# First MLP products as seven products of blocks, with three of four weight sums made by adding transfers

## The chip, the cores and the metric

The kernel runs on one core of a Trainium2 chip. The core has a matrix engine (TensorE, PE in the profile; its weight loads are listed as PEld), three engines for elementwise work (VectorE = DVE, ScalarE = ACT, GpSimd = POOL), and SyncE (SP), which here only issues transfers. Each engine works through its own instructions in the order of the program, and semaphores make one engine wait for another. Transfers issued by SP's queue are plain copies; POOL's queue can also issue adding transfers, which add what they fetch to what stands in SBUF. The metric is device time of one execution in microseconds.

## The reference

A two-layer encoder on x of 512 positions and 1024 features, in float32: layer 0 has stick-breaking attention, layer 1 an RG-LRU block, and each is followed by the same kind of MLP. Cut to the part that the change touches:

```python
def squared_relu_mlp(h, w1, w2):
    u = jax.nn.relu(h @ w1)          # 512x1024 @ 1024x4096
    return (u * u) @ w2              # 512x4096 @ 4096x1024
...
    h = rms_norm(x, norm_mlp[layer])
    x = x + squared_relu_mlp(h, mlp_w1[layer], mlp_w2[layer])
return rms_norm(x, norm_final)
```

## The kernel before

**Precision.** TensorE multiplies in a format shorter than float32 (float32r). So every operand is kept as a high part and a low part, `a = ah + al`: ScalarE copies it to the high part, which rounds it (the CAST of lines 197, 823 and 843), and VectorE subtracts that from the original for the low part (lines 204, 824, 844). One product is then three matmuls, high x high, high x low and low x high. In this text "cut" is that pair of operations on a block of weights, giving `wh` and `wl`, and "split" the same on u.

**The MLP.** Class `Mlp` handles one layer. The 4096 hidden features are done in four quarters of 1024 (`q4`, 0 to 3). Each quarter has a first product (x with w1, relu, square: u) and a second product (u with w2, added up in the four output tiles c0 to c3). x lies feature by position: `xgh` and `xgl` are the halves of x times the norm's factors. The norm's other factor, one number per position, is put in when results are collected (`rr`, line 888), so relu and square can run before it is known.

- First product, before: `squared(q4, c)` makes 128 features of u at a time: it fetches a slab of 512 KB of weights, cuts it, and does 8 x 3 matmuls of 512 columns (lines 209 to 211), 8 such per quarter.
- Second product: `down()` uses Strassen's scheme in Winograd's form: of 2 x 2 blocks it makes seven products P1 to P7 instead of eight, with sums of blocks as operands. A quarter has two pairs (units of 512 features, index g or p), so 14 products of 12 matmuls of 512 columns each (line 877). The sums of u are made by `sums()` (line 807) and split by `split()`; the sums of weights are made in place: P5 is b11+b12, P6 adds b22 to that, P7 is b12+b22, P4 adds b21 to P6's sum. VectorE adds them (line 865), except where a product stands in `far`: there POOL issues an adding transfer (line 858). Before, `far` has P7 and P4 in the last quarter of layer 0, P4 in the last of layer 1, and is empty elsewhere.
- `block()` forms the sum and `operand()` cuts it into `wh` and `wl`, which come from a pool of four buffers: an operand can be cut once the product four before it is done. `load()` fetches b11, b12 and b22 (two buffers each, one for each pair) on SP's queue; b21 is fetched where it is needed, into one of three raw buffers.
- u of two chunks stands in one tile (line 787) of which there is one buffer, so the next two chunks can write theirs only after the split; the splits go to `bh`/`bl` for the first pair and to `sh`/`sl` for the second.
- `quarters()` runs it all: the eight chunks of a quarter, then `down()`; the first two chunks of the next quarter are put ahead of `down()`.

**Order.** TensorE's order is that of the program text. The order on the other engines is chosen by a scheduler, when the program is built; once built, it is fixed. x of each layer stays in SBUF (`HOMES`) until the second product's output is added to it: in layer 0 by `feature()`, in layer 1 by transposes in `between()` in the last quarter (lines 1189 to 1195).

Of the kernel before, what the change touches and what calls it, by code (L numbers as in the profile page):

```python
# [14 lines left out]
ALU = mybir.AluOpType  # L15
# [33 lines left out]
def hybrid_encoder(  # L49
# [10 lines left out]
    w_m1: bass.AP,  # L60
    w_dn: bass.AP,
# [666 lines left out]
    class Mlp:  # L728
# [10 lines left out]

        PRODUCTS = {  # L740
            "P1": (0, "b11", None, "X", 0, False),
            "P5": (4, "b11", "b12", "V", 3, False),
            "P6": (5, "b11", "b22", "X", 1, True),
            "P3": (6, "b22", None, "V", 1, False),
            "P7": (1, "b12", "b22", "X", 3, True),
            "P2": (2, "b21", None, "W", 0, False),
            "P4": (3, "b11", "b21", "X", 2, False),
# [5 lines left out]
        def __init__(self, ctx, layer):  # L753
# [9 lines left out]
            self.u, self.raws = {}, {}  # L763
# [9 lines left out]
        def squared(self, q4, c, ready=None):  # L773

            if self.first is None:
                self.first = [self.bank() for _ in range(2)]
                ws = [slab(w_m1[self.layer, i]) for i in range(2)]
                beside(ws, xgh, xgl, self.first, {})
            if self.first:
                ps = self.first.pop(0)  # L780
            else:
                ps = dense(
                    w_m1[self.layer, q4 * C + c], xgh, xgl, halves=ready, ps=self.bank()
                )
            j, a = divmod(c, 2)
            if a == 0:
                self.u[j] = self.mp.tile([P, BLOCKS, HS], F32, tag="u", name="u", bufs=1)
            t = self.u[j][:, 2 * a : 2 * a + 2, :].rearrange("p i n -> p (i n)")
            A.activation(t, ps, AF.Relu)
            A.activation(t, t, AF.Square)  # L790
            if q4 == 0:

                if c in range(2, C - 2):
                    for i in range(2):
                        self.sq.chunk(2 * (c - 2) + i, x[2 * (c - 2) + i])
                if c == C - 1:
                    self.rr = self.sq.inv_squares(self.bank())
            return t

        def sums(self, j):  # L800

            u = self.u[j]
            for out, x, y, op in (
                (4, 1, 3, ALU.subtract), (5, 4, 0, ALU.subtract), (6, 5, 2, ALU.add),
                (1, 0, 1, ALU.subtract),
            ):
                V.tensor_tensor(u[:, out, :], u[:, x, :], u[:, y, :], op)  # L807

        def split(self, j):
            if j < 2:  # L810
                n = BLOCKS * HS
                h, l = (
                    t.rearrange("p c s -> p (c s)")[:, j * n : (j + 1) * n].rearrange(
                        "p (i n) -> p i n", n=HS
                    )
                    for t in (bh, bl)
                )
            else:
                h, l = (
                    self.bp.tile([P, BLOCKS, HS], F32R, tag=t, name=t) for t in ("sh", "sl")  # L820
                )
            u = self.u[j]
            A.copy(h, u)  # L823
            self.ready = V.tensor_tensor(l, u, f(h), ALU.subtract)  # L824
            self.a[j] = h, l

        def weights(self, q4, g, tag):
            return w_dn[self.layer, q4, g, *self.SOURCES[tag]]

        def load(self, q4):  # L830

            for g in range(2):
                for tag in ("b11", "b12", "b22"):
                    t = self.bp.tile([P, 2, S], F32, tag=tag, name=tag)
                    nc.sync.dma_start(out=t, in_=self.weights(q4, g, tag))
                    self.raws[tag, g] = t
# [10 lines left out]
        def block(self, q4, name, g, far):  # L847

            _, b, to, *_ = self.PRODUCTS[name]
            if b == "b21":  # L850
                t = wpool.tile([P, C, P], F32, tag="raw", name="raw", bufs=3)
                t = t.rearrange("p (j k) f -> p j (k f)", j=2)
                nc.sync.dma_start(out=t, in_=self.weights(q4, g, b))
                self.raws[b, g] = t
            raw = self.raws[b, g]
            if name in far:

                G.dma_start(out=raw, in_=self.weights(q4, g, to), accum_op=ALU.add)  # L858
            elif to:

                ahead = None
                if far and (name, g) != ("P5", 0):
                    ahead = self.ready if name == "P5" else self.before
                with tc.issue_after(ahead.ins) if ahead else nullcontext():
                    self.sum = V.tensor_tensor(raw, raw, self.raws[to, g], ALU.add)  # L865
            return self.operand(raw)

        def times(self, name, g, i, w, ps, new, cols=slice(0, S)):
# [4 lines left out]
            for jj in range(2):  # L873
                h, l = self.a[2 * g + jj]
                first, last = new and g == jj == 0, g == jj == 1
                for n, (x, y) in enumerate(((h, wh), (h, wl), (l, wh))):
                    PE.matmul(  # L877
                        ps, x[:, block, ts], y[:, jj, cols], start=first and n == 0,
# [14 lines left out]
        def down(self, q4, far=(), end=None):  # L893
            sums, last_cut = {}, {}

            def product(name, g, w=None):
                w = w or self.block(q4, name, g, far)
# [13 lines left out]
            if end is None:  # L911
                for name in ("P1", "P5", "P6", "P3", "P7", "P2", "P4"):
                    for g in range(2):
                        product(name, g)
# [414 lines left out]
```

## Time and profile before

| what | value |
| --- | --- |
| time, median of 3 runs | 1076.51 us (1075.07 to 1077.06) |
| the profiled execution: time / span | 1076.9 us / 1075.1 us |
| TensorE's granted clock, mean over the span | 0.997 |
| transfers, mean over the span | 117 GB/s |
| adding transfers in the MLPs / in layer 1's RG-LRU stage | 6 / 10 |
| MLP of layer 0 / layer 1, from the first quarter's second product to the end of the last | 304.4 to 576.4 us / 788.6 to 1075.1 us |

How to read it: busy time of an engine is the sum of its instructions; TensorE's matmuls are pipelined, so one lasts longer than the distance to the next, and a pace is read from the distance of starts. A row of the windows gives the stretch, then for each engine its busy time and count of instructions, the granted clock, the mean busy share of the 16 transfer engines and the GB/s moved. A row of a group gives line, engine, operation, `output<-inputs`, shapes, count, busy time, mean ns of one, then the idle time of the engine ahead of them and what ended it. A row of the timeline gives start, duration, engine, line and operation.

### The profile page before, as it was taken

To read this page: it belongs to the slowest core of one execution; us is meant where nothing else is said; L and a number is where in the kernel's file an instruction comes from. 1 tells how busy PE (TensorE), PEld (TensorE's weight loads), DVE (VectorE), ACT (ScalarE), POOL (GpSimd) and SP (SyncE) were. 2 spreads that over 40 slices of the span, in tenths; PEclk is the share of its full clock that TensorE was granted. 3 is DMA by queue.
4 is the path that set the end of the run, shared out by engine and by line. 5 is a ranking of instruction groups with operands and counts; after the bars stand their busy time and mean duration, and the time that the engine had idled before them with its cause. 6 is when DMAs were issued, how large, how long until landed. Compare 5 with 4: busy or idle time off the path is not lost.

```text
span 1075.1 us, 13570 instructions
## 1 busy us (share of the span) xinstructions
PE 1059.4 (99%) x5004; PEld 879.4 (82%) x5004; DVE 782.4 (73%) x1020; ACT 599.6 (56%) x888; POOL 166.8 (16%) x192
## 2 busy tenths in 40 slices
PE   9999999999999999999999999999999999999997
PEld 7888888888888888888878777888888888888875
DVE  7788787838686596597578878974676597497667
ACT  6777676826554543544546477944554544544346
POOL 2344443510000000000001655000000000000005
PEclk9999999999999999999999999999999999999999
DMA  7745454517215206206341785252215206305104
GB/s 236 198 117 148 122 147 108 170 52 249 85 49 187 79 31 187 96 20 191 84 98 60 180 211 129 87 191 82 79 43 190 82 22 189 103 20 176 59 6 112
DMA packets 44033, 125.70 MB, mean 117 GB/s; under 512 B 7744, under 2 KB 8512, under 8 KB 43968
## 3 DMA queue, kind: packets, MB, share of 16 engines
q1 hardware_dynamic: 41088, 115.94, 34.8%
q0 software_dynamic: 2304, 8.39, 4.5%
q8 instruction: 39, 0.64, 0.2%
q10 hardware_dynamic: 576, 0.52, 0.1%
q14 instruction: 26, 0.21, 0.1%
HBM read 104.91 MB, written 2.10 MB: 100 GB/s over the span
## 4 chain that ended last, share of the span: by engine, by line
PE 86%; DVE 5%; ACT 3%; issue 2%; POOL 2%; DMA 1%; SPq 0%; ACTq 0%; DVEq 0%; POOLq 0%
PE ps_t L877 8%; PE ps_acc L877 7%; PE ps_o L877 6%; PE ps_acc L211 6%; PE ps_acc L209 6%; PE ps_acc L210 6%; PE ps_z L877 5%; PE ps_t L209 4%; PE ps_t L210 4%; PE ps_t L211 4%; PE ps_o L209 4%; PE ps_o L211 4%; PE ps_o L210 4%; PE ps_z L210 3%; PE ps_z L211 3%; PE ps_z L209 3%
## 5 line engine op out<-in xcount | busy, mean ns | idle before, releaser
L204 DVE TENSOR_TENSOR wl<-raw,wh 128x1024 fp32r<-128x1024 f32 (+2 forms) x126 | 130.5, 1052 | 89.7 <-ACT wh L197 89.5
L843 ACT CAST wh<-b 128x1024 fp32r<-128x1024 f32 x96 | 100.0, 1048 | 122.2 <-PE ps_t L877 23.3
L197 ACT CAST wh<-raw 128x1024 fp32r<-128x1024 f32 (+2 forms) x136 | 119.5, 898 | 66.9 <-PE ps_acc L877 10.2
L844 DVE TENSOR_TENSOR wl<-b,wh 128x1024 fp32r<-128x1024 f32 x96 | 116.5, 1221 | 41.6 <-ACT wh L843 40.9
L209 PE MATMUL ps_acc<-xgh,wh 128*128 128x512 f32 x288 | 116.0, 403 | 1.0 <-ACT wh L178 0.9
L210 PE MATMUL ps_acc<-xgh,wl 128*128 128x512 f32 x288 | 112.7, 391 | 0.3 <-DVE wl L179 0.3
L211 PE MATMUL ps_acc<-xgl,wh 128*128 128x512 f32 x288 | 112.6, 391 | 0.1
L858 POOL DMA_DIRECT2D b<-in_w_dn x6 | 5.4, 904 | 680.9 <-DVE wl L844 358.7
L209 PE MATMUL ps_t<-xgh,wh 128*128 128x512 f32 x200 | 78.7, 394 | 0.0
L210 PE MATMUL ps_t<-xgh,wl 128*128 128x512 f32 x200 | 78.0, 390 | 0.0
L211 PE MATMUL ps_t<-xgl,wh 128*128 128x512 f32 x200 | 77.8, 389 | 0.0
L561 DVE TENSOR_TENSOR_SCAN scan<-keep,later 128x128 f32<-128x128 f32 (+1 forms) x64 | 58.4, 916 | 17.6 <-ACT keep L551 10.8
L211 PEld LDWEIGHTS ps_acc<-xgl,wh 128*128 128x128 f32 x288 | 54.1, 188 | 12.0 <-DVE xgl L118 0.5
L209 PE MATMUL ps_o<-xgh,wh 128*128 128x512 f32 x160 | 63.1, 394 | 0.2 <-DVE x L713 0.2
L209 PEld LDWEIGHTS ps_acc<-xgh,wh 128*128 128x128 f32 x288 | 54.2, 188 | 10.9 <-ACT wh L178 1.1
L211 PE MATMUL ps_o<-xgl,wh 128*128 128x512 f32 x160 | 62.3, 390 | 0.0
L210 PE MATMUL ps_o<-xgh,wl 128*128 128x512 f32 x160 | 62.3, 389 | 0.0
L210 PEld LDWEIGHTS ps_acc<-xgh,wl 128*128 128x128 f32 x288 | 54.3, 188 | 9.6 <-DVE wl L179 1.0
L565 POOL TENSOR_TENSOR w<-w,scan 128x128 f32<-128x128 f32 (+1 forms) x64 | 53.5, 838 | 52.5 <-DVE scan L561 49.5
L865 DVE TENSOR_TENSOR b<-b,b 128x1024 f32<-128x1024 f32 x46 | 56.1, 1222 | 0.9
L807 DVE TENSOR_TENSOR u<-u 128x256 f32<-128x256 f32 x128 | 49.5, 419 | 0.7
L824 DVE TENSOR_TENSOR bl<-u,bh 128x1792 fp32r<-128x1792 f32 x16 | 32.4, 2025 | 22.9 <-ACT bh L823 22.9
(332 smaller groups left out, 2761.6 us busy)
## 6 DMA issues: line engine op xcount, KB each, us to landing
raw<-in_w_m SPq DMA_DIRECT2D x64, 512.0 KB, 3.5
b<-in_w_dn SPq DMA_DIRECT2D x48, 512.0 KB, 3.6
raw<-in_w_dn SPq DMA_DIRECT2D x16, 512.0 KB, 3.5
raw<-in_w_in SPq DMA_DIRECT2D x16, 512.0 KB, 4.0
raw<-in_w_qk SPq DMA_DIRECT2D x12, 512.0 KB, 3.5
wl<-raw POOLq DMA_DIRECT2D x10, 512.0 KB, 6.2
x<-in_xT SPq DMA_DIRECT2D x16, 256.0 KB, 4.2
raw<-in_w_ro SPq DMA_DIRECT2D x8, 512.0 KB, 4.3
```

What stands on the lines that cost most here:

```text
L197: A.copy(wh[:, k, :], raw[:, k, :])
L204: V.tensor_tensor(wl[:, k, :], raw[:, k, :], f(wh[:, k, :]), ALU.subtract)
L209: PE.matmul(ps, wh, ah, start=start, stop=False)
L210: PE.matmul(ps, wl, ah, start=False, stop=False)
L211: PE.matmul(ps, wh, al, start=False, stop=stop)
L561: V.tensor_tensor_scan(sc[:, S - n : S][:, ::-1], keep[:, :n][:, ::-1], later[:, S - n :][:, ::-1], 1.0, ALU.mult, ALU.max,)
L565: G.tensor_tensor(wt, wt, sc[:, S - n + 1 : S + 1], ALU.mult)
L807: V.tensor_tensor(u[:, out, :], u[:, x, :], u[:, y, :], op)
L843: A.copy(wh, raw)
L844: self.cut = V.tensor_tensor(wl, raw, f(wh), ALU.subtract)
L865: self.sum = V.tensor_tensor(raw, raw, self.raws[to, g], ALU.add)
L877: PE.matmul(ps, x[:, block, ts], y[:, jj, cols], start=first and n == 0, stop=last and n == 2, skip_group_check=not new,)
```

## The change

The first products of quarters 1 to 3 are made by the same seven-product scheme as the second. Quarter 0 keeps its slabs.

- `up(q4, p)`, new, makes the u of one pair: seven products of 24 matmuls of 256 columns. Its moving operands are blocks and sums of blocks of x (`xa`), its weights come as blocks from `w_up` through the same `block()`. P1, P5 and P6 are copied out of PSUM by ScalarE (`kept`); P3, P7 and P2 are combined with a kept one by VectorE; then relu and square. P4 goes on in the PSUM bank of P1, P6 and P7.
- The sums of x are made once per layer in quarter 0: `sums_of_x()` in place on x, `halves_of_sums()` for their halves. x itself is overwritten by that. In layer 0 it is stored to DRAM before (`between`) and fetched again ahead of the last `down()` (`back`); in layer 1 it is transposed into the output tiles in quarter 0 already, by ScalarE.
- `u` is now one tile per pair with four slots, still with one buffer; the split is cut in three pieces, the first one ahead of the sums.
- Of the four weight sums of a pair, three in `up()` (P5, P7, P4) and two in `down()` (P7, P4) are made by adding transfers (`FAR_UP`, `FAR_DOWN`). The last `down()` of each layer keeps its own lists.
- `down()` takes its products in other orders (`ORDERS`), and the factors of the final norm (`gb`) are fetched late, into freed tiles of x.

```diff
+        def up(self, q4, p, unit, far):
+            u = self.u_tile(p)
+            banks, kept = {}, {}
+            for name in ("P1", "P5", "P6", "P3", "P7", "P2", "P4"):
+                w = [t.rearrange("p j n -> p (j n)") for t in self.block(unit, name, far)]
...
+                for i in range(2):
+                    for k in range(C // 2):
+                        h, l = self.xa(block, k)
+                        wh, wl = (t[:, k, i * P : (i + 1) * P] for t in w)
+                        for n, (m, y) in enumerate(((wh, h), (wl, h), (wh, l))):
+                            PE.matmul(
+                                ps[:, i * HS : (i + 1) * HS], m, y,
...
+                if name in ("P1", "P5", "P6"):
+                    t = work.tile([P, S], F32, tag="sq" if name == "P1" else "r", name="kept")
+                    A.copy(t, ps)
...
+                slot, one, op = {
+                    "P3": (1, "P6", ALU.subtract), "P7": (2, "P5", ALU.subtract),
+                    "P2": (0, "P1", ALU.add), "P4": (3, None, None),
+                }[name]
+                t = u[:, :, slot, :]
+                if name == "P3":
+                    V.tensor_tensor(t, three, kept[one], op)
+                elif one:
+                    V.tensor_tensor(t, kept[one], three, op)
+                A.activation(t, t if one else three, AF.Relu)
+                self.square(t)
+                if name == "P2":
+                    self.split(p, slice(0, 2), slice(0, 3), slice(0, 3))
+            self.sums(p, slice(0, 2))
+            for i in range(2):
+                self.split(p, i, slice(0, 4), slice(3, 7))
```

```diff
+        def u_tile(self, p):
+            if p not in self.u:
+                self.u[p] = self.mp.tile([P, 2, 4, HS], F32, tag="u", name="u", bufs=1)
+            return self.u[p]
...
+        def sums_of_x(self, k):
+            lo, hi = slice(0, HS), slice(HS, S)
+            u, v = x[k], x[C // 2 + k]
+            for c in (k, C // 2 + k):
+                g = col(f"mlp{self.layer}")[:, c : c + 1]
+                A.activation(x[c], x[c], AF.Identity, scale=g)
+            V.tensor_tensor(v[:, hi], u[:, hi], v[:, hi], ALU.subtract)
+            V.tensor_tensor(u[:, hi], u[:, lo], u[:, hi], ALU.subtract)
+            V.tensor_tensor(u[:, lo], v[:, hi], u[:, lo], ALU.subtract)
+            V.tensor_tensor(v[:, lo], u[:, lo], v[:, lo], ALU.add)
```

```diff
-            if name in far:
-                G.dma_start(out=raw, in_=self.weights(q4, g, to), accum_op=ALU.add)
+            if to and name in far:
+                G.dma_start(
+                    out=raw.rearrange("p j n -> p (j n)"), in_=unit["src"](to), accum_op=ALU.add
+                )
...
+        ORDERS = {
+            "first": "P1 0 P5 0 P2 0 P1 1 P5 1 P6 0 P6 1 P3 0 P3 1 P7 0 P7 1 P2 1 P4 0 P4 1",
+            "mid": "P1 0 P5 0 P1 1 P2 0 P5 1 P6 0 P6 1 P3 0 P3 1 P7 0 P7 1 P2 1 P4 0 P4 1",
+            "last": "P1 0 P5 0 P2 0 P1 1 P2 1 P5 1 P6 0 P6 1 P3 0 P3 1 P7 0 P7 1 P4 0 P4 1",
+        }
...
+        FAR_UP, FAR_DOWN = ('P5', 'P7', 'P4'), ('P7', 'P4')
...
+            for q4 in range(NQ):
+                if q4:
+                    del self.u[0], self.u[1], self.a[1]
+                    for p in range(2):
+                        self.up(q4, p, units[p], self.FAR_UP)
+                        units[p] = self.from_down(q4, p)
+                last = q4 == NQ - 1
+                if last:
+                    end.ready()
+                    self.down(q4, units, far, end)
+                    break
+                self.down(q4, units, self.FAR_DOWN)
+                if q4 == 0:
+                    self.replace()
+                units = [self.from_up(q4 + 1, p) for p in range(2)]
```

More of the change, by code (lines that the diff above doesn't have):

```diff
@@ L781, in squared @@
             else:
[L782 to L822, printed above, removed]
+                ps = dense(w_m1[self.layer, c], xgh, xgl, ps=self.bank())
```

252 lines of the change are left out of this document (184 added, 68 removed).

## The prediction

> **What bounds the kernel now.** I read the page first (span, busy shares, chain of waits), then the windows of the MLP quarters, then the timeline of TensorE for the pace of its matmuls.
>
> ```profile
> span 1075.1 us, 13570 instructions
> PE 1059.4 (99%) x5004; PEld 879.4 (82%) x5004; DVE 782.4 (73%) x1020; ACT 599.6 (56%) x888; POOL 166.8 (16%) x192
> PE 86%; DVE 5%; ACT 3%; issue 2%; POOL 2%; DMA 1%; SPq 0%; ACTq 0%; DVEq 0%; POOLq 0%
> 342.70:386.22 43.52, 43.52 (x194) 36.04 (x192) 26.93 (x30) 20.38 (x24) 0.00 (x0) 1.00 0.23 74
> 386.22:424.48 38.26, 38.26 (x169) 31.54 (x168) 30.39 (x34) 18.21 (x19) 0.00 (x0) 1.00 0.44 137
> 827.26:870.78 43.52, 43.52 (x193) 36.04 (x192) 26.87 (x30) 20.39 (x24) 0.00 (x0) 1.00 0.23 73
> 870.78:909.47 38.69, 38.69 (x170) 31.53 (x169) 30.48 (x34) 18.22 (x19) 0.00 (x0) 1.00 0.43 136
> 538.91:576.38 37.47, 36.49 (x158) 28.93 (x157) 29.97 (x33) 16.06 (x16) 2.62 (x3) 1.00 0.38 84
> 342.70 0.39 PE L209 MATMUL ps_o<-xgh,wh 128*128 128x512 f32 x1
> 386.22 0.39 PE L877 MATMUL ps_o<-wh,bh 128*128 128x512 f32 x1
> ```
>
> TensorE is the bound, at full granted clock (1.00). A first product (the window from 342.70) has 192 matmuls of 512 columns in 43.52 us, 0.2267 us each. A second product has 168 in 38.26 us in layer 0 and 38.69 us in layer 1, so 2.73 us for each group of 12. Neither waits. Only the last second product of a layer does: 156 matmuls at 0.2278 us are 35.5 us of its 37.47 us. VectorE is busy 57 of 82 us, ScalarE 39 of 82: there is room, if the new work falls where it can be done in time.
>
> **What the change removes and adds on TensorE.** Six first products (three quarters, two layers) turn from 192 matmuls of 512 columns into 2 pairs x 7 products x 24 = 336 of 256 columns. The kernel has such matmuls already:
>
> ```profile
> 40.03 0.28 PE L458 MATMUL ps_t<-wh,xgh 128*128 128x256 f32 x1
> 42.06 0.28 PE L460 MATMUL ps_t<-wh,xgl 128*128 128x256 f32 x1
> 40.04 0.19 PEld L459 LDWEIGHTS ps_t<-wl,xgh 128*128 128x128 f32 x1
> ```
>
> They are 18 in a row, 17 gaps in 2.03 us: 0.119 us each, though a weight load lasts 0.19 us; loads and matmuls overlap. So a product of blocks takes 24 x 0.119 = 2.85 us and a first product 14 x 2.85 = 39.9 us, 3.6 us less than 43.52. Six times that is 21.7 us: all that the change can win.
>
> [...]
>
> **What the other engines must do in those 39.9 us.** The durations:
>
> ```profile
> L844 DVE TENSOR_TENSOR wl<-b,wh 128x1024 fp32r<-128x1024 f32 x48 | 58.3, 1221 | 19.4 <-ACT wh L843 18.9
> L865 DVE TENSOR_TENSOR b<-b,b 128x1024 f32<-128x1024 f32 x22 | 26.9, 1222 | 0.4
> L824 DVE TENSOR_TENSOR bl<-u,bh 128x1792 fp32r<-128x1792 f32 x8 | 16.2, 2025 | 11.6 <-ACT bh L823 11.6
> L843 ACT CAST wh<-b 128x1024 fp32r<-128x1024 f32 x48 | 50.0, 1047 | 61.2 <-PE ps_t L877 11.6 <-PE ps_acc L877 9.2 <-DVE b L865 8.6
> L789 ACT ACTIVATE u<-ps_o 128x512 f32<-128x512 f32 x9 | 5.4, 596 | 11.0 <-PE ps_o L211 8.7 <-DVE sl L824 1.1 <-DVE bl L824 1.1
> L790 ACT ACTIVATE u<-u 128x512 f32<-128x512 f32 x32 | 19.7, 633 | 0.3
> 1040.01 1.22 DVE L844 TENSOR_TENSOR wl<-b,wh 128x1024 fp32r<-128x1024 f32 x1
> 1041.14 1.22 DVE L865 TENSOR_TENSOR b<-b,b 128x1024 f32<-128x1024 f32 x1
> 1004.11 0.69 DVE L1195 TENSOR_TENSOR c<-c,ps_o 128x512 f32<-128x512 f32 x1 [3.92 <-PE ps_o L1192]
> 1004.71 0.68 DVE L1195 TENSOR_TENSOR c<-c,ps_t 128x512 f32<-128x512 f32 x1
> ```
>
> A "cut" (operand: wh on ScalarE 1.05, then wl on VectorE 1.22) lasts 2.3 us. In a row VectorE starts one 1024-column operation each 1.14 us and one of 512 columns each 0.6; the split of 1536 columns I put at 1.65 us (from 1024 and 1792), that of 768 at 0.9, a 256-column sum at 0.4. Per pair VectorE has 7 cuts, 1 weight sum, 3 combinations from PSUM, 4 sums of u and splits of 1536 and 2 x 1024 columns: 8.0 + 1.1 + 1.8 + 2.4 + 1.65 + 2.3 = 17.3 us of 19.95. ScalarE has 7 casts, 3 kept copies, 4 relu and square and the split copies, some 16 us. Throughput would suffice. What remains is the order, and there the adding transfers count:
>
> ```profile
> L858 POOL DMA_DIRECT2D b<-in_w_dn x6: 862/881/1027, 528.6 to 1048.8; - x6
> DMA to landing us min/median/max: 5.3/5.4/5.5
> 1047.13 1.21 DVE L844 TENSOR_TENSOR wl<-b,wh 128x1024 fp32r<-128x1024 f32 x1
> 1048.75 0.87 POOL L858 DMA_DIRECT2D b<-in_w_dn  x1 [2.42 <-DVE wl L844]
> b<-in_w_dn SPq DMA_DIRECT2D x48, 512.0 KB, 3.6
> ```
>
> From the end of the cut that frees its block (1048.34) to POOL's issue is 0.41 us, to the landing 5.4: 5.8 us, where the sum on VectorE that it replaces takes 1.22. P5, P6 and P4 all add into b11, so in up() these lie in one chain: cut P1, add, cut P5, sum, cut P6, add, cut P4. In the changed program's order both ScalarE and VectorE have the cut of the second pair's P1 behind that of the first pair's P4, so the second pair's chain hangs on the end of the first's. At its end P4 of the second pair waits on TensorE for the combination of P7 (L933, same PSUM bank), which VectorE has behind the cut of P4, the splits of the first pair's u (there is one u buffer) and two cuts of down().
>
> Added up, with T = 0 where TensorE could start the first P1:
> - P4 of the down() before needs the operand buffer of the product four before, free 5 groups earlier at -13.65; cut -11.3; reload of b11 3.6: -7.7; cut of P1 behind two collects: -4.9.
> - add 5.8: 0.9; cut P5: 3.2; collect and sum: 5.0; cut P6: 7.3; add: 13.1; cut P4: 15.4.
> - Second pair: combination 0.6 and cut of P1 1.14: 17.2; add: 23.0; cut P5: 25.3; sum 1.1, split 1.65, cut P6: 29.2; add: 35.0; cut P4: 37.3.
> - sum 0.6, cut, split, sum, split, cut (5 x 1.14 and hand-overs), two combinations 1.2: 44.8. Then 24 matmuls: 47.7.
>
> So a first product ends at 47.7 us, not at 39.9: 4.2 us later than the 43.52 of today, six times 25.2 us. Small stalls of TensorE inside (P5, P6: about 1 us each) are contained in it.
>
> **Price of an add beside other traffic.** Before, adds ran almost alone. Beside many transfers the same kind took longer:
>
> ```profile
> L201 POOL DMA_DIRECT2D wl<-raw x10: 892/906/1237, 596.4 to 654.1; - x10
> DMA to landing us min/median/max: 4.5/6.2/9.0
> q1 hardware_dynamic: 41088, 115.94, 34.8%
> q0 software_dynamic: 2304, 8.39, 4.5%
> ```
>
> A load of 512 KB takes all 16 engines 1.69 us (34.8% of 1075 us over 221 such), an add 3.0 us (4.5% over 16); a quarter has 16 loads and 10 adds, 57 us of some 85. The two adds for P4 fall beside the reloads of b22 and b12; I take 5.8 us for them, between 5.4 and the 6.2 of that stage: 0.4 x 2 x 6 = 4.8 us. Bounds for all four: 4.5 us (21.6 less) and 6.2 us (19.2 more).
>
> [...]
>
> **Where the second product then waits.** Its P5 of the second pair, due 10.9 us after the start, needs sums and splits of u that can only begin when P4 of that pair is squared (about 4.5 us after 47.7). VectorE then has weight sums, cuts and collects among them: in quarter 1 of both layers and quarter 2 of layer 1 nine operations lie before the splits, the split ends 1.4 us late; in quarter 2 of layer 0 eleven, and the split ends 3.8 us late. Together 8.0 us. The last quarters have it later in their order; their 2 us of waiting stand today too: 0.
>
> **First quarter of each layer.** Its first product keeps its 192 matmuls; VectorE gets 16 sums and 12 low halves of x (about 11.5 us). u has one buffer for both pairs, so the second pair's relu waits for the first's splits. In layer 0, from the start of down() VectorE has 5 cuts, 2 weight sums, four splits and 8 sums of u in front of P5's operands (5.7 + 2.3 + 4.0 + 3.2, from 0.5): 15.7, so P5 ends at 17.3 and not 13.65: 3.7 us. In layer 1 x can be summed only after the last transposes, 15 us before down(); some 32 us of VectorE work follow, P5 ends at 19: 5.4 us. Sum 9.1; bounds 0 and 15.
>
> The stores of x (8 x 256 KB) and their reload lie beside matmuls; the residual adds on VectorE that layer 1 loses (8 x 0.68) were hidden. Transposes only move: 0. Reloading x ahead of b11 on SP's queue delays an operand due 8 us later by some 2 us: 0, up to 2.
>
> **Sum.** 1076.9 us (the profiled run, 1075.1 of span and 1.8 around it) + 25.2 + 4.8 + 8.0 + 9.1 = 1124.0; against the median of 1076.51 shown that is 1123.6.
>
> **Rivals.**
> - *The chain is covered and TensorE bounds (faster).* An add would have to land in 3.4 us: four times 2.0 less ends the chain at 39.7. Then 1076.9 - 21.7 + 17.1 of waits in down() = 1072.3, without those waits 1055. For it: VectorE has 13% of its time free. Against: no add in the trace landed under 4.5 us. Chance 0.10.
> - *Weight loads bound the 256-column matmuls.* 336 x 0.19 = 63.8 us instead of 43.52: six times 20.3 more, about 1199. Only the 0.19 us speaks for it, the pace of 0.119 against: 0.02.
> - *Congested adds.* If all land like the slowest of L201, 9.0 us: 3.6 x 4 x 6 = 86 more on top of 1119, about 1205. For it: 57 of 85 us of transfer time; against: the median of 6.2. Chance 0.04.
> - That the new matmuls are not there can be ruled out: the program's TensorE stream grows by 864 = 6 x 144.
>
> **How the numbers follow.** The forecast itself has 0.82, and slower with the two heavier cases 0.88; faster 0.10; within 0.2% (2 us, about what a measurement of this kernel can tell from no change) 0.02. Range: adds at 4.5 us and no waits in the first quarters give 1124.0 - 4.8 - 21.6 - 9.1 = 1088; all adds at 6.2 and 15 us in the first quarters give 1124.0 - 4.8 + 19.2 + 5.9 = 1144. I take 1087 to 1146.
>
> **What would show it.** Right: first products of about 48 us in quarters 1 to 3, TensorE idle just ahead of the second pair's P4 (released by VectorE) and of its P5 (released by an add), POOL's adds landing in 5 to 6.5 us, 256-column matmuls 0.119 us apart where they do not wait. Wrong: first products of 40 us without gaps; or gaps in the first pair as long as in the second, with adds over 8 us.

## The result, and the profile after

The changed kernel takes 1191.09 us (median of four executions, 1185.16 to 1191.73) where the kernel before takes 1076.72: 1.1058 times as long, with a 95% interval of 1.1024 to 1.1092. The forecast was 1124, with a range up to 1146. The direction was right, the size was not: 114 us more instead of 47. The profiled execution took 1185.16 us, with a span of 1183.2 us, so it stands at the lower end of the four.

From the page of the kernel after, first the span, the engines and the chain of waits, then the transfers (size of one, median us to landing) and the share of POOL's queue:

```profile
span 1183.2 us, 15809 instructions
PE 1078.6 (91%) x5868; PEld 929.8 (79%) x5868; DVE 852.6 (72%) x1108; ACT 676.0 (57%) x1025; POOL 215.3 (18%) x252
...
q0 software_dynamic: 10944, 39.85, 20.1%
...
DMA b<-in_w_up 7%; PE ps_z L1004 2%; PE ps_acc L1004 2%; ACT wh L971 1%; DVE wl L972 1%; PE ps_o L1004 1%; PE ps_t L913 1%; PE ps_t L1004 1%; DVE u L835 1%; DVE b L991 1%; DVE sl L826 1%; PE ps_z L913 0%; DVE c L1015 0%; DVE u L931 0%; ACT u L934 0%
...
b<-in_w_dn SPq DMA_DIRECT2D x48, 512.0 KB, 5.5
b<-in_w_up SPq DMA_DIRECT2D x36, 512.0 KB, 5.3
b<-in_w_up POOLq DMA_DIRECT2D x36, 512.0 KB, 5.9
```

TensorE fell from 99% busy to 91%, and a transfer, the weights of the first products, now leads the chain of waits. (The page could follow that chain back only to 881 us, so it covers layer 1's quarters 1 to 3 alone.) An adding transfer lands in 5.9 us, close to the 5.8 us of the forecast; but plain reloads of the same 512 KB went from 3.6 us to over 5.

The windows of the kernel after, by stage; after the length come busy times and counts of PE, PEld, DVE, ACT and POOL, then the granted clock of TensorE, the share of the transfer engines and GB/s:

```profile
293.21:334.88 41.67, 38.81 (x169) 31.39 (x168) 30.81 (x56) 20.73 (x24) 4.35 (x5) 1.00 0.65 152
334.88:393.01 58.13, 45.15 (x338) 43.70 (x336) 35.38 (x36) 32.36 (x41) 4.36 (x5) 0.91 0.47 118
393.01:431.94 38.93, 38.77 (x171) 31.35 (x169) 27.99 (x31) 15.54 (x16) 4.36 (x5) 1.00 0.69 176
431.94:489.95 58.01, 46.52 (x337) 45.03 (x337) 37.80 (x38) 31.83 (x40) 4.36 (x5) 0.89 0.49 119
489.95:533.43 43.48, 40.63 (x169) 32.65 (x169) 29.88 (x32) 15.59 (x17) 4.36 (x5) 0.95 0.64 157
533.43:590.42 56.99, 45.15 (x337) 43.72 (x336) 34.78 (x36) 31.77 (x40) 4.37 (x5) 0.88 0.59 161
...
834.36:881.64 47.28, 40.97 (x169) 32.26 (x168) 34.40 (x45) 17.38 (x20) 5.19 (x6) 0.93 0.61 144
881.64:938.22 56.58, 46.10 (x338) 44.82 (x336) 36.38 (x36) 31.78 (x40) 4.11 (x5) 0.88 0.50 121
977.51:1037.20 59.69, 45.45 (x337) 43.79 (x336) 38.09 (x39) 31.67 (x40) 4.96 (x6) 0.91 0.47 115
1076.48:1133.15 56.67, 44.70 (x337) 43.34 (x336) 34.19 (x36) 31.68 (x40) 3.42 (x4) 0.94 0.44 112
```

The rows with 336 weight loads (x336, once x337) are the six first products: 56.6 to 59.7 us each, 57.7 on average, where 47.7 was forecast and 43.52 is the stage before. The first row and the one from 834.36 are the second products of the first quarters (41.67 and 47.28 us), those from 393.01 and 489.95 two of the four of quarters 1 and 2. The granted clock of the first products is 0.88 to 0.94, not 1.00: that was in no step of the prediction. The trace's clock records put 87 us at half clock, against 8 us before; here and below such sums hold some 2 us behind the last instruction.

Where the 108.1 us between the two profiled spans (1183.2 and 1075.1) lie, from windows like these, with the forecast beside them:

| stage | forecast | measured |
| --- | --- | --- |
| six first products (25.2 + 4.8) | +30.0 | +85.0 |
| second products of quarters 1 and 2, four | +8.0 | +7.1 |
| second products of the first quarters (layer 0 + layer 1) | 3.7 + 5.4 | 3.4 + 8.6 |
| last quarters' second products, to the last matmul | 0 | +0.6 and +2.5 |
| everything else (the 32 transposes that move from the last quarter of layer 1 to its first are set off) | 0 | +1.0 |

So 55 of the 61 missing microseconds lie in the first products. Quarter 2 of layer 0, whose first matmul TensorE starts at 431.94, without a wait behind the second product, in the timeline of the kernel after (start, duration, engine, line, operation; in brackets the idle time and what ended it):

```profile
417.73 0.86 POOL L986 DMA_DIRECT2D b<-in_w_up  x1 [9.79 <-DMA b<-in_w_up]
420.34 0.87 POOL L986 DMA_DIRECT2D b<-in_w_up  x1 [1.74 <-DMA b<-in_w_up]
420.80 3.04 SPq L948 DMA_DIRECT2D b<-in_w_up  x2
430.70 1.05 ACT L971 CAST wh<-b 128x1024 fp32r<-128x1024 f32 x1 [8.48 <-DMA b<-in_w_up]
431.78 1.23 DVE L972 TENSOR_TENSOR wl<-b,wh 128x1024 fp32r<-128x1024 f32 x1 [5.73 <-ACT wh L971]
433.41 0.86 POOL L986 DMA_DIRECT2D b<-in_w_up  x1 [12.20 <-DVE wl L972]
438.97 1.05 ACT L971 CAST wh<-b 128x1024 fp32r<-128x1024 f32 x1 [7.23 <-DMA b<-in_w_up]
445.87 0.86 POOL L986 DMA_DIRECT2D b<-in_w_up  x1 [11.59 <-DVE wl L972]
452.75 2.00 ACT L971 CAST wh<-b 128x1024 fp32r<-128x1024 f32 x2 [2.70 <-DMA b<-in_w_up]
462.78 1.05 ACT L971 CAST wh<-b 128x1024 fp32r<-128x1024 f32 x1 [4.06 <-DMA b<-in_w_up]
485.90 0.36 PE L913 MATMUL ps_z<-xgh,wh 128*128 128x256 f32 x1 [3.04 <-ACT u L934]
```

and the landing times of the two reloads issued from 420.80, from the view of their line (minimum, median, maximum):

```profile
DMA to landing us min/median/max: 8.3/9.1/9.8
```

SP issues the reloads of both b11 at 420.80 and 423.5; the first is there 9.8 us later, and its cast starts at 430.70. Just ahead of it POOL had issued two adds, those for P7 of the coming first product. So the cut of P1, which the forecast had done 4.9 us ahead of TensorE, is done 1.1 us after it (433.0), 6.0 us late. This is the latest of the six: over all of them the reload for the first pair takes 7.5 to 9.8 us, and the cut is done between 1.5 us ahead of TensorE and 1.1 us after it, 4.8 us late on average. From there the chain is the forecast one: 433.41 the add for P5, 438.97 its cast, 445.87 the add for P4, 452.75 its cast, 462.78 the cast of the second pair's P5, and P4 of the second pair starts at 485.90. From the cut of P1 to the start of the second pair's P4 it was to take 49.7 us and took 52.9.

What the clock does there, in the same timeline, at the first pair's P5:

```profile
440.07 0.58 PE L913 MATMUL ps_acc<-s,wh 128*128 128x256 f32 x1 [4.00 <-ACT wh L971]
441.33 0.58 PE L913 MATMUL ps_acc<-s,wl 128*128 128x256 f32 x1 [0.68 <-DVE wl L972]
441.71 0.42 PE L913 MATMUL ps_acc<-low,wh 128*128 128x256 f32 x1
441.93 0.41 PE L913 MATMUL ps_acc<-s,wh 128*128 128x256 f32 x1
442.14 0.41 PE L913 MATMUL ps_acc<-s,wl 128*128 128x256 f32 x1
442.35 0.41 PE L913 MATMUL ps_acc<-low,wh 128*128 128x256 f32 x1
```

After 4 us of idling the matmuls come 0.21 us apart and no longer 0.119. Counted over the six first products, their 346.1 us are 239.5 us of matmuls at 0.119, 80.9 us of gaps and 25.8 us that the slow matmuls take beyond that pace. In e5 below, shorter idle stretches, of 2.8 to 2.9 us, were followed by half clock too, in all six first products. In the clock records of the changed kernel half clock comes in stretches of 3.41 or 6.83 us, but for the last one, which runs on behind the last instruction (5.14 us).

### The profile page after: what moved, and what is told of

It reads as the page before. It is cut to its first block, busy times and chain, and to the rows that moved or that the text cites. A ratio compares the mean times of both kernels' runs of the same rounds, so it can differ in the third digit from the quotient of the medians.

```text
span 1183.2 us, 15809 instructions
## 1 busy us (share of the span) xinstructions
PE 1078.6 (91%) x5868; PEld 929.8 (79%) x5868; DVE 852.6 (72%) x1108; ACT 676.0 (57%) x1025; POOL 215.3 (18%) x252
## 5 line engine op out<-in xcount | busy, mean ns | idle before, releaser
L971 ACT CAST wh<-b 128x1024 fp32r<-128x1024 f32 x168 | 172.1, 1048 | 276.7 <-DMA b<-in_w_up 142.8
L972 DVE TENSOR_TENSOR wl<-b,wh 128x1024 fp32r<-128x1024 f32 x168 | 203.6, 1222 | 172.2 <-ACT wh L971 171.9
L198 ACT CAST wh<-raw 128x512 fp32r<-128x512 f32 (+2 forms) x88 | 69.5, 818 | 37.3 <-DMA raw<-in_w_in 10.5
L205 DVE TENSOR_TENSOR wl<-raw,wh 128x512 fp32r<-128x512 f32 (+2 forms) x78 | 71.4, 941 | 16.4 <-ACT wh L198 16.3
L913 PE MATMUL ps_t<-xgh,wh 128*128 128x256 f32 x144 | 44.5, 309 | 19.3 <-ACT u L934 17.9
L991 DVE TENSOR_TENSOR b<-b,b 128x1024 f32<-128x1024 f32 x46 | 55.7, 1220 | 0.3
L913 PE MATMUL ps_z<-xgh,wh 128*128 128x256 f32 x144 | 42.6, 296 | 8.8 <-ACT u L934 7.6
L835 DVE TENSOR_TENSOR u<-u 128x512 f32<-128x512 f32 (+1 forms) x80 | 46.4, 581 | 0.6
L212 PEld LDWEIGHTS ps_acc<-xgl,wh 128*128 128x128 f32 x208 | 39.1, 188 | 8.9 <-DVE xgl L119 0.5
L913 PE MATMUL ps_t<-xgh,wl 128*128 128x256 f32 x144 | 43.9, 305 | 1.2 <-DVE wl L972 1.2
L913 PE MATMUL ps_t<-low,wh 128*128 128x256 f32 x160 | 44.8, 280 | 0.0
L210 PEld LDWEIGHTS ps_acc<-xgh,wh 128*128 128x128 f32 x208 | 39.3, 189 | 6.5 <-ACT wh L179 0.5
L972 DVE TENSOR_TENSOR wl<-raw,wh 128x1024 fp32r<-128x1024 f32 x28 | 34.2, 1223 | 12.9 <-ACT wh L971 12.7
```

The costliest lines, as they stand in the source:

```text
L198: A.copy(wh[:, k, :], raw[:, k, :])
L205: V.tensor_tensor(wl[:, k, :], raw[:, k, :], f(wh[:, k, :]), ALU.subtract)
L210: PE.matmul(ps, wh, ah, start=start, stop=False)
L212: PE.matmul(ps, wh, al, start=False, stop=stop)
L835: V.tensor_tensor(u[:, i, out, :], u[:, i, x, :], u[:, i, y, :], op)
L913: PE.matmul(ps[:, i * HS : (i + 1) * HS], m, y, start=new and i == k == n == 0, stop=i == 1 and k == C // 2 - 1 and n == 2, skip_group_che ...
```

## Experiments

Each table row gives the median, the ratio to the kernel before with its interval, the mean of the six first products and of the four second products of quarters 1 and 2 (from windows), and the mean granted clock of the profiled execution.

| kernel | us | ratio | first | second | clock |
| --- | --- | --- | --- | --- | --- |
| before | 1076.7 | 1 | 43.5 | 38.5 | 0.997 |
| changed | 1191.1 | 1.1058 [1.1024, 1.1092] | 57.7 | 40.2 | 0.964 |
| e1 spare matmuls | 1192.5 | 1.1081 [1.1063, 1.1100] | 55.2 | 44.1 | 0.979 |
| e2 adds for P5, P4 | 1175.9 | 1.0913 [1.0884, 1.0942] | 56.0 | 39.3 | 0.967 |
| e3 adds for P7 | 1113.3 | 1.0342 [1.0326, 1.0358] | 44.7 | 40.2 | 0.980 |
| e4 no adds | 1126.4 | 1.0470 [1.0454, 1.0486] | 46.6 | 40.2 | 0.976 |
| e5 adds for P7, P4 | 1100.5 | 1.0223 [1.0206, 1.0240] | 44.2 | 39.1 | 0.982 |
| e6 adds for P5, P7 | 1154.9 | 1.0727 [1.0711, 1.0743] | 53.3 | 39.1 | 0.969 |
| e7 as e3, kept in place | 1138.2 | 1.0572 [1.0556, 1.0587] | 39.7 | 50.8 | 0.969 |
| e8 as e7, first order | 1134.3 | 1.0533 [1.0517, 1.0549] | 39.7 | 50.8 | 0.972 |
| e9 as e5, kept in place | 1106.4 | 1.0286 [1.0269, 1.0303] | 39.8 | 43.7 | 0.980 |
| e10 as e5, new orders | 1100.5 | 1.0227 [1.0209, 1.0245] | 43.6 | 40.9 | 0.986 |
| e11 as e9, new orders | 1111.6 | 1.0329 [1.0314, 1.0344] | 39.7 | 46.0 | 0.983 |
| e12 as e11, last too | 1107.4 | 1.0290 [1.0275, 1.0306] | 39.8 | 46.1 | 0.983 |
| e13 as e5, 8 spare | 1102.6 | 1.0247 [1.0233, 1.0261] | 42.9 | 40.3 | 0.992 |
| e14 as e5, 16 spare | 1114.1 | 1.0358 [1.0341, 1.0375] | 42.6 | 43.2 | 0.986 |
| e15 as e13, first order | 1101.9 | 1.0231 [1.0216, 1.0247] | 42.6 | 42.1 | 0.992 |

### Which adding transfer costs what (e2 to e6)

The edit is the lists of products whose sums are made by adds (the run stands behind `#`):

```diff
-        FAR_UP, FAR_DOWN = ('P5', 'P7', 'P4'), ('P7', 'P4')
+        FAR_UP, FAR_DOWN = ('P5', 'P4'), ('P4',)          # e2
+        FAR_UP, FAR_DOWN = ('P7',), ('P7',)               # e3
+        FAR_UP, FAR_DOWN = (), ()                         # e4
+        FAR_UP, FAR_DOWN = ('P7', 'P4'), ('P7', 'P4')     # e5
+        FAR_UP, FAR_DOWN = ('P5', 'P7'), ('P7', 'P4')     # e6
```

> The sums for P7 go back to VectorE in up() and down(); those for P5 and P4 stay adding transfers. Theory A (the adds for P7, issued just as b11 is fetched again, make that fetch late, 9.8 us instead of 3.6, and the whole chain of a first product starts late by it): the reload of b11 lands in under 6.5 us, the cut of the first P1 is done at most 1 us after TensorE is ready for it instead of 1.1 to 3 us after, the gaps per first product fall from 13.5 to 8 to 10 us, and the time falls by 20 to 30 us, to about 1160. Rival (VectorE has no room, the late start is its own queue): two more sums per first product and second product on VectorE take as much as they give, gaps stay at 13 us or grow, time 1180 or more.

> Only the sums for P7 are made by adding transfers; P5 and P4 are summed by VectorE in up(), P4 in down(). Theory B (the two adds in the chain of each pair, 5.8 us each where VectorE takes 1.2, set the gaps): the chain of a first product is 4 x 4.6 = 18.4 us shorter, more than the 13.5 us of gaps, so the gaps fall under 4 us, the half clock goes with them, VectorE (19.6 us per pair of TensorE's 19.95) is the next bound, first products of 42 to 46 us and a time of 1090 to 1115. Rival (the gaps come from VectorE's order: splits, combinations and cuts behind each other, with the adds only beside them): first products stay over 52 us, time over 1150.

> No adding transfers in up() or in the second products of quarters 0 to 2; all weight sums by VectorE. Theory B: as with P7 alone, gaps small, but VectorE has 20.7 us of work per pair for 19.95 us of TensorE, so first products of 43 to 48 us, time 1095 to 1120, a few us above the version with P7 by adds. Theory A adds that loads land in about 4 us again. Rival (VectorE's room is the reason why adds are needed): VectorE is over 85% busy in the first products and they last over 52 us, time over 1150.

> As the changed kernel, but in up() P5's sum is made by VectorE; P7 and P4 stay adding transfers. Theory B1 (the prediction's chain: both adds of a pair lie in it, P4's too since the second pair's first cut stands behind the cut of P4): one of two links goes, 4.6 us twice per first product, 55 us in all, 1130 to 1145, first products of 49 to 51 us. Theory B2 (only P5's add counts, since P4 is needed four products later and its add hides): nearly all of the gain of taking both back, 1110 to 1122, first products under 47 us. Theory A's part (late reload beside P7's adds) would leave it above either: reload landings of 6 us and more.

> As the changed kernel, but in up() P4's sum is made by VectorE; P5 and P7 stay adding transfers. B1: the same gain as for P5, 1130 to 1145. B2: the gaps ahead of P5 stay, 1175 to 1190.

Theory B held for pace and time: with P7 alone by adds (e3) the first products are 44.7 us and the time 1113. The half clock did not go with the gaps, as it had expected: one of 3.4 us is left ahead of the second pair's P4, and 23 us of the six first products still lie at half clock. e4 missed its range by 6 us, on the side that VectorE's work was expected to push to.

Theory A held in its cause and missed in its price. Without the adds for P7 (e2) the reload of b11 lands in 3.4 to 4.7 us in all six quarters; in the quarter of layer 0 shown above, both reloads:

```profile
DMA to landing us min/median/max: 3.5/4.1/4.6
```

The cut of the first P1 is then done 2.5 to 4.3 us ahead of TensorE, on average 3.0 us earlier than in the changed kernel. (The expectation read that kernel's cuts as 1.1 to 3 us late; they are done between 1.5 us ahead and 1.1 us late.) But the second pair's P4 starts only 2.1 us earlier, the gaps go from 13.5 to about 12.4 us and not to 8 to 10, the first products are 1.7 us shorter, and the time falls by 15 us, not 20 to 30. The chain of P5 and P4 stays, and VectorE has two sums more in each first and second product; that these sums take the rest is argued, not shown.

e5 against e6 parts the two adds of the chain, which the prediction had priced alike. Taking back P5's add alone is worth 91 us (1191.1 to 1100.5), P4's alone 36 us (to 1154.9); beside e3, P4's add even helps: e5, with it in both lists, is 13 us faster. So P4's add hides behind the products ahead of it, once P5's is gone; e5 came out below the ranges of B1 and B2, nearer to B2, and e6 lies between the two. The reloads, which were expected to stay late in e5 since P7's adds are still there, land early. And P5's add costs more than its own link. Why is in the timeline of e5, with the reload of b11 and the add for P7 in quarter 2 of layer 0 (TensorE starts at 419.22):

```profile
408.07 3.04 SPq L948 DMA_DIRECT2D b<-in_w_up  x2
416.43 0.88 POOL L986 DMA_DIRECT2D b<-in_w_up  x1 [21.20 <-DVE b L991]
```

and in the landing times of those two reloads, from the view of their line in the same stretch (minimum, median, maximum):

```profile
DMA to landing us min/median/max: 3.4/3.5/3.5
```

In all six quarters of e5 they land in 3.4 to 4.2 us.

The add for P7 changes b12 in place. Where VectorE makes P5's sum it reads b12 from SBUF, so the add for P7 has to wait for that sum (416.43, released by `DVE b L991`), 8 us behind the reload. Where POOL makes P5's sum, the transfer fetches b12 from DRAM again, nothing holds the add for P7 but the landing of b12 itself (417.73 and 420.34 in the changed kernel, released by `DMA b<-in_w_up`), and it goes out just ahead of the reload. In e6, with adds for P5 and P7, the reloads take 5.8 to 9.6 us again; in quarter 3 of layer 0:

```profile
DMA to landing us min/median/max: 8.1/8.9/9.6
```

### What the lowered clock costs (e1, e13, e14)

```diff
+        def idle(self, ps, n):
+            for _ in range(n):
+                PE.matmul(
+                    ps[:, :HS], xgh[:, 0, :P], xgh[:, 0, :HS], start=True, stop=True,
+                    skip_group_check=True,
+                )
...
+                if (name, p) == ("P5", 0):
+                    self.idle(ps, 32)              # e1 alone
+                if (name, p) == ("P4", 1):
+                    self.idle(self.bank(), 28)     # e1; 8 in e13, 16 in e14
```

> The changed kernel with 32 spare matmuls of 256 columns ahead of the first pair's P5 and 28 ahead of the second pair's P4 in every up(), where TensorE idled 3.2 to 4.7 us; they read only halves of x that stand ready, and nothing reads their results. Theory C (TensorE's idle stretches of over 3 us are what halves its granted clock afterwards): the half clock, 87 us in the changed kernel, goes almost wholly from the first products (what stays hangs on gaps elsewhere, under 30 us), the mean granted clock rises from 0.964 to over 0.985, and the time falls by 10 to 26 us: 26 us were lost at half clock in the six first products, less what the later waits had hidden anyway. Rival (the clock falls with the kind of matmul or with the load, not with idling): granted clock 0.96 as now, and the time the same 1185 to 1192 or longer by the spare matmuls that find no gap.

> P5's sum by VectorE, P7 and P4 by adds, and 8 spare matmuls of 256 columns (0.95 us) in the 2.9 us gap ahead of the second pair's P4 in every first product. Theory C (idle stretches of nearly 3 us and more are followed by 3.4 us or more of half clock, which costs TensorE real time where nothing else waits behind it): an idle stretch of about 1.9 us no longer drops the clock, the 1.4 to 2.4 us of slow matmuls at the end of each first product and the 0.5 us at the start of the second go, time 1100.5 less 8 to 14: 1087 to 1093. Rival C2 (what half clock costs is hidden, since another engine sets the end of each quarter): clock up, time within 3 us of 1100.5. Rival C3 (the clock does not follow the gap): half clock as before, 40 us.

> The same with 16 spare matmuls (1.9 us). Theory C: the clock as with 8, the gap filled further, no more to win: within 3 us of the run with 8. C2: 1100.5 again. If filling is paid for (the spare matmuls end later than the gap): slower than with 8 by up to 6 us.

In e1 half clock fell from 87 to 53 us (in the six first products from 67 to 9) and the first products by 2.5 us each, but the second products took 3.9 us more, and the time stayed. The spare matmuls also moved the order that the scheduler gives ScalarE and VectorE, so e1 does not settle the price. In e13 that order moved less: a dozen operations of VectorE and four of ScalarE changed places. The spare matmuls also take a PSUM bank of their own, which shifts the banks of the products behind them. Windows of e5 and then of e13, a first and a second product of each layer:

```profile
336.34:380.27 43.93, 41.17 (x337) 40.99 (x336) 34.36 (x35) 31.74 (x40) 3.47 (x4) 0.96 0.61 152
380.27:419.22 38.95, 38.78 (x170) 31.39 (x169) 32.92 (x36) 16.55 (x17) 3.48 (x4) 1.00 0.58 151
839.08:883.24 44.16, 41.48 (x338) 41.30 (x337) 35.32 (x36) 30.84 (x39) 3.47 (x4) 0.96 0.60 150
883.24:922.52 39.28, 39.10 (x170) 31.41 (x169) 32.55 (x35) 16.57 (x17) 3.46 (x4) 1.00 0.57 149
```

```profile
335.48:377.84 42.36, 40.63 (x345) 40.46 (x344) 33.08 (x34) 30.45 (x40) 3.47 (x4) 1.00 0.63 158
377.84:417.86 40.02, 38.86 (x170) 31.40 (x169) 33.34 (x36) 17.42 (x18) 3.48 (x4) 1.00 0.56 146
841.03:883.81 42.78, 41.06 (x346) 40.89 (x344) 34.24 (x35) 29.86 (x39) 3.47 (x4) 1.00 0.62 155
883.81:924.22 40.41, 39.33 (x171) 31.41 (x169) 33.78 (x37) 17.42 (x18) 3.46 (x4) 1.00 0.56 146
```

Eight spare matmuls (0.95 us) bring the first products' clock from 0.96 to 1.00 and half clock in the whole span from 41 to 21 us: the clock does follow the gap (C3 falls). The first product is 1.4 to 1.6 us shorter, the second product 1.1 us longer, and the time is 1102.6 against 1100.5: rival C2 in the time. In the second products of quarters 1 and 2 TensorE now waits for VectorE's split of the second pair's u, 0.9 to 1.3 us in each of the four, where in e5 it waits 0.2; the first of them in e13:

```profile
390.40 0.50 PE L1013 MATMUL ps_o<-wh,sl 128*128 128x512 f32 x1 [1.00 <-DVE sl L826]
```

So there TensorE's slow matmuls had stood in time in which the next product would have waited anyway. In all, the six first products gained 8.4 us, the four second products behind them gave 4.6 back, and those of the last quarters took 4.9 us more, with a wait for a cut of about 2 us each that e5 does not have. That last loss may come from the moved order; without it, up to 4 us of the gain might have stayed, so e13 shows that more than half of it is hidden and not that all is. e14, expected within 3 us of e13 or up to 6 us slower, moved the orders as e1 did and is 11.5 us slower; it says nothing on the clock's price.

### What sets the pace when the adds are out of the chain (e7 to e12, e15)

```diff
                 if name == "P3":
-                    V.tensor_tensor(t, three, kept[one], op)
+                    V.tensor_tensor(kept[one], three, kept[one], op)
                 elif one:
-                    V.tensor_tensor(t, kept[one], three, op)
-                A.activation(t, t if one else three, AF.Relu)
+                    V.tensor_tensor(kept[one], kept[one], three, op)
+                A.activation(t, kept[one] if one else three, AF.Relu)
```

```diff
-            "first": "P1 0 P5 0 P2 0 P1 1 P5 1 P6 0 P6 1 P3 0 P3 1 P7 0 P7 1 P2 1 P4 0 P4 1",
+            "first": "P1 0 P5 0 P2 0 P1 1 P2 1 P6 0 P5 1 P6 1 P3 0 P3 1 P7 0 P7 1 P4 0 P4 1",
```

The first edit is in e7, e8, e9, e11 and e12, the order in e8 and e15 (first quarter), in e10 and e11 (quarters 0 to 2) and in e12 (all). e7 and e8 have the adds of e3, the others those of e5; e15 has the 8 spare matmuls.

> P7 alone by adds, as before, and the combinations of P3, P7 and P2 are written into the kept copy in place of u, so that they need not wait for the one u buffer. Theory D (the 3.4 us gap that is left ahead of the second pair's P4 is the wait for the first pair's splits to free u, and the half clock follows it): the gap falls under 1 us, the half clock in the first products with it, first products of 40 to 42 us instead of 44.7, time 1113 less 15 to 30: 1083 to 1098. Rival (VectorE has no room): the wait moves into the second product, ahead of its P5, and the time stays above 1106.

> As the one with combinations in place, and in the first quarter's second product P5 of the second pair is taken two products later (P1 0, P5 0, P2 0, P1 1, P2 1, P6 0, P5 1 and on). Theory E (TensorE waits there, 4.8 us in layer 0 and 7.3 us in layer 1, with half clock behind it, only because the splits of the second pair's u are late by less than two products of 2.73 us): the gaps there fall under 2 us, and the time is 9 to 15 us less than without the new order. Rival (VectorE is behind with all of its work there, sums of x among it): the gap moves to a later product, and the time differs by under 4 us.

> P7 and P4 by adding transfers (P5 by VectorE), combinations in the kept copies, second products in their old orders. Theory F (with the combinations out of the way TensorE runs first products in 39.5 us, and the second pair's split is then simply late for a second product that asks for it as fifth): first products 39.5 us without gaps, second products of quarters 1 and 2 of 45 to 50 us with waits for the split ahead of P5 of the second pair, time 1100 to 1130. Rival (with P4's sums off VectorE it has the room): second products under 42 us, time under 1085.

> P7 and P4 by adds, combinations written to u as in the changed kernel, and in the second products of quarters 0 to 2 P5 of the second pair two products later. Theory E (in quarter 0 the split is late by less than two products): the waits of quarter 0 go (2.9 us in layer 0, more with half clock in layer 1), the other quarters stay, time 1100 less 8 to 15: 1085 to 1093. Rival (VectorE is behind there with everything): under 4 us of difference.

> P7 and P4 by adds, combinations in place, P5 of the second pair two products later in quarters 0 to 2. Theory F: the first product keeps its 39.5 us and the later P5 gives the split the 5.5 us that it lacks, second products of 39 to 42 us: 6 x 4.4 us less than with P5's sum alone taken back, less 10 us in quarter 0, time 1062 to 1082, at or under the kernel before. Rival (VectorE's and ScalarE's work per quarter is the bound by now, near 72 us of 78): the waits move on to P6 or P3 of the second pair, time over 1095.

> As the one before, and the last second product of each layer in the same order. Theory F: the same wait of the last quarter (some 3 us each) goes too: 2 to 8 us less. Rival: the last quarters' order on VectorE is tied to the products by hand, and the change of order costs there as much as it gives: within 2 us, or slower.

> With 8 spare matmuls and, in the first quarter alone, P5 of the second pair two products later. Theories C and E together: 8 to 14 us by the clock and 4 to 6 us by the order (second product of quarter 0 of layer 0 43.3 to 40.5 us, of layer 1 47.8 to 45.7): 1082 to 1090, still over the 1076.7 of the kernel before, since its first products are 42 us at best against 43.5 and the first quarter still costs some 9 us.

e7 shows the prediction's floor with nothing in the way, and where the wait went; its windows of a first and a second product, and the wait in that second product's P5:

```profile
338.81:378.27 39.46, 39.46 (x337) 39.45 (x336) 32.04 (x33) 26.58 (x33) 1.75 (x2) 1.00 0.50 133
378.27:428.41 50.14, 41.56 (x170) 32.62 (x169) 39.48 (x42) 20.92 (x24) 1.72 (x2) 0.93 0.40 105
```

```profile
397.38 0.79 PE L1004 MATMUL ps_z<-wh,sh 128*128 128x512 f32 x1 [5.19 <-ACT sh L825]
```

336 matmuls in 39.46 us are 0.117 us each, without a gap and at full clock. The second product then waits 5.2 us for the split of the second pair's u and takes 50.1 us. Theory D was right about the cause of the gap (the combinations wait for the one u buffer) and its rival right about the time: 25 us more than e3. e8, expected 9 to 15 us below e7, is 4 us below it, as its rival had it.

e9 expected 1100 to 1130 and took 1106, though its second products (43.7 us) came out shorter than expected. The theories of a later P5 fell: e10, expected at 1085 to 1093, stays at 1100.5, and e11, expected at 1062 to 1082, is 5 us above e9. The second products of the first quarters did gain (43.3 us in e5 to 40.6 in e10 in layer 0, 47.8 to 45.7 in layer 1), but those of quarters 1 and 2 lost 1.8 us each on average, for the split that P5 of the second pair needs came later too. From e9 to e11 it came later by as much as it was asked for later. VectorE's half of it, in the timeline of e9 (second product from 377.09) and of e11 (from 373.64):

```profile
391.88 2.36 DVE L826 TENSOR_TENSOR sl<-u,sh 128x1024 fp32r<-128x1024 f32 x2 [0.46 <-ACT sh L825]
```

```profile
393.62 2.36 DVE L826 TENSOR_TENSOR sl<-u,sh 128x1024 fp32r<-128x1024 f32 x2
```

It begins 14.8 us into the second product in e9 and 20.0 us into it in e11, 5.2 us later for a P5 that TensorE takes two products of 2.73 us later: with the new order other cuts stand ahead of it on VectorE. e12 (4 us less than e11, as expected) and e15 (expected at 1082 to 1090, no gain on e13) change nothing in this. A first and a second product together take 83.4 us in e5, 83.1 in e13 and 83.5 in e9, wherever the wait stands, 84.6 in e10 and 85.7 in e11, and 82.0 in the kernel before.

No version tried reaches the kernel before; the nearest are e5, e10 and e15, 2.2 to 2.3% slower. Most of what is left stands in the first quarters, whose first products keep their matmuls while VectorE gets the sums of x; no run here changes that work. Of the 23.1 us between the profiled spans of e5 and of the kernel before, 14.1 lie in their second products (43.3 and 47.8 us for 38.3 and 38.7), 4.3 in the six first products and 2.6 in the second products of quarters 1 and 2.

## Why the prediction was right or wrong

- **Pace of the 256-column matmuls: right.** 39.9 us of TensorE in a first product; e7 has 39.46 without a gap. That is 0.117 us for each matmul, less than the 0.19 us of the weight load in the prediction's rows. Matmuls and loads were both busy through all of that window (39.46 and 39.45 us), so they overlapped in the first products too.
- **The chain through b11: right in kind, and the loss.** From the cut of P1 to the second pair's P4 it took 52.9 us for 49.7. Its two links were not alike: P4's add, priced at 4.6 us above VectorE's sum like P5's, costs nothing once P5's is gone (e5 against e3).
- **The step that failed: "reload of b11 3.6: -7.7; cut of P1 behind two collects: -4.9".** The reload took 9.8 us in the quarter shown and 7.5 to 9.8 in the six, and the cut of P1 was done at +1.1 instead of -4.9 (-1.5 to +1.1 in the six). The contention term of 4.8 us was given to the adds for P4 alone; the adds for P7 were counted as transfers but not placed. Making P5's sum by a transfer frees the add for P7 to go out right at that reload, and e5 and e6 show it. Of 10.3 us by which the quarter shown missed, 6.0 are this late start, 3.2 the longer chain, and 1.2 the last 24 matmuls, half of them at half clock. Over the six it is 4.8, 3.5 and 1.7 of 10.0 us. These are the forecast's own terms, measured along its chain; taking the P7 adds away alone gave back less (e2: 3.0 us of the late start, 1.7 us of a first product), since other work moved with them.
- **"Small stalls of TensorE inside (P5, P6: about 1 us each) are contained in it": wrong as put.** The stall at the first pair's P5 is 2.7 to 4.2 us and another 1.1. Most of it is the late start seen from TensorE: in e2, with the reload early, it is at most 1.8 us and 1.1. The prediction named gaps in the first pair as long as in the second as a sign against it, with adds over 8 us. In the quarter shown they are as long (6.6 and 6.7 us), in the other five shorter (4.1 to 7.6 against 8.2 to 8.6); the adds land in 5.9 us (median), and those for P7, issued just ahead of the reloads, in 6.1 to 10.5.
- **Granted clock: missing.** The prediction let every matmul run at 1.00. Slow matmuls add 25.8 us to the six first products. How much of that the changed kernel really pays was not isolated; in e13, a faster kernel, taking them away did not shorten the time.
- **Waits in second products: size right, place wrong.** 7.1 us for 8.0, with 5.2 of it in quarter 2 of layer 0 (3.8 forecast) and 0.6 to 0.7 in each of the others (1.4 forecast).
- **First quarters: layer 0 right (3.4 us for 3.7), layer 1 short** (8.6 for 5.4): its wait for the last split is 5.6 us, with half clock behind it.
- **Last quarters: 0 forecast, 3.1 measured.** The rival of a covered chain fell. The one of congested adds fell as it was put, since adds land in 5.9 us and not in 9; the congestion was in the reloads and in the adds for P7 issued just ahead of them.

## What to carry to other kernels

An operation moved from an engine to a transfer also drops the waits that it imposed on others: look for what may now start earlier, and what it will collide with. Price a chain by its start as well as by its links, with every transfer that is in flight at that moment. A wait that is cured on the bounding engine is won only if the engines feeding it have work done ahead; where order on them is chosen when the program is built, changing TensorE's order moves theirs too.

## What the hardware showed that was not expected

- TensorE's granted clock fell to half behind short gaps. In e5 an idle stretch of 2.8 to 2.9 us ahead of the second pair's P4 in each first product was followed by matmuls 0.21 us apart, where they had come at 0.119, in all six; filled to leave 1.72 to 1.73 us, it was not in any (e13). In e10 gaps of 2.9 and 3.1 us passed twice without it, so in these runs the length alone did not decide.
- A plain reload of 512 KB on SP's queue takes 3.4 to 3.5 us (e5, quarter 2 of layer 0, no add in flight), and 8.3 to 9.8 us behind two adding transfers of the same size issued 3.1 and 0.5 us ahead of the first reload (the changed kernel, same quarter). The adds of the first products land in 5.9 us (median); those two take 9.2 and 10.5 us.
- Half the clock can cost little: the time of e5 did not fall when half of its 41 us at half clock was taken away (1100.5 us, and 1102.6 in e13, which has 21 us at half clock and in which some operations also changed places).
